# Two transformer blocks on one core: the opening reordered, half of the memory keys moved to the first output stage

## The chip, the cores and the metric

The kernel runs on one core of a Trainium2 chip. The metric is the device time of one execution in microseconds (us). The core has five engines that run side by side, each through its own list of instructions in order: TensorE (PE: matmuls, with its weight loads PEld), VectorE (DVE), ScalarE (ACT), GpSimd (POOL) and SyncE (SP, which here only issues DMAs). Engines wait for each other through semaphores. TensorE writes its results into banks of PSUM; the other engines read them from there into SBUF.

## What is computed

Two blocks follow each other for 512 tokens (S) of width 1024 (D). What matters here is the start of the first block and the memory branch of the second:

```python
def first_block(x, c, positions, w_ada, b_ada, g_pre, w_in, ...):
    mod = silu(c) @ w_ada + b_ada                  # one row of 3 * 1024
    shift, scale, gate = split(mod, 3)
    h = rms_norm(x, g_pre) * (1 + scale) + shift
    proj = h @ w_in                                # qa ka va fa za qb kb vb zb
    oa = forgetting_attention(qa, ka, va, fa + b_fgate) * silu(za)
    ob = sliding_window_sink_attention(rope(qb), rope(kb), vb, sinks) * silu(zb)
    y = concat([oa, ob]) @ w_out
    return x + gate * rms_norm(y, g_post)

def second_block(x, mem, ...):
    h = rms_norm(x, norm_g); mem_h = rms_norm(mem, mem_norm_g)   # mem: 256 tokens
    ...                                            # conv branch, differential attention
    k, v = split(mem_h @ w_mem_kv, 2)              # memory keys and values, 1024 columns each
    k = rms_norm(k per head of 256, kn_g)
    y_mem = (softmax(q @ k.T / 16) @ v * silu(gate)) @ w_proj
    ...
    return x + (g0 * y_conv + g1 * y_diff + g2 * y_mem) @ w_out
```

## The kernel before

**Products.** Most products are made from two halves of each number, a rounded one (`hh`, `wh`: fp32r) and the rest (`hl`, `wl`), as three matmuls: high by high, high by low, low by high. `load_w` (L157) fetches a weight matrix in raw tiles on the SP queue, ACT casts each piece to `wh` (L170), and DVE or POOL subtracts to get `wl` (L172). `mm_T`, `mm_N` and `mm_W` (L202, L213, L221) issue the three matmuls for each of the eight contraction chunks of 128. A few products of the opening are made in plain fp32 instead, where TensorE runs each matmul as two passes: the profile counts a pass as one matmul.

**Order.** In the opening every instruction on PE, ACT, DVE and POOL goes through `Ordered` (L342), which keeps the written order on each engine, so the whole opening shows as line 342. Elsewhere a scheduler places instructions by priority, and may slip them between those of the opening. SP issues DMAs in the written order there.

**The opening** (L346 to L520). It has four strands.

- Memory: `mt` (256 memory tokens) is transposed into `mT`; two chunks of 512 memory-key columns, `mem_k(0)` and `mem_k(1)`, are multiplied in plain fp32 (16 matmuls, so 32 passes each) from raw tiles `rawm` into two PSUM banks `sc`, scaled by ACT into `mk`. `mT` is also written to `mT_d` in memory by a DMA on ACT's queue.
- Tokens: `xn` (512 tokens of 1024) is fetched, its squares summed on ACT, scaled on DVE, transposed by 32 TensorE transposes (`mm<-cst,xn`) and copied by ACT into `xt`.
- Modulation: `w_ada` for shift and scale comes as eight chunks `ada` of 1 MB. For a chunk either ACT and DVE form the products (`products`: two ACT instructions, six of DVE and an add) and TensorE sums over partitions (`sums`: two matmuls with a single column, tile `acc`), or TensorE does all of it (`sums_pe`: 16 matmuls with a single column, tile `ada`). Before, chunks 5 and 7 go the second way. `modulate` makes `mod` and `gs` (0.16 us each on DVE).
- Hidden: `hidden(k)` makes `hh[k]` on ACT, `ht` on DVE and `hl[k]` on POOL (DVE for the last two).

The DMAs are issued on SP in this order: `mt`, the first key chunk's four raw tiles, `ada` 0 and 1, `xn`, two raw tiles of the second key chunk, `ada` 2 and 3, and the rest as buffers come free.

**The first projection** (L644 to L649), `w1c` with 264 columns (kb, vb and the forget gate), follows: 96 matmuls, the token tile outermost, one bank for each of the four token tiles in turn. ACT copies each into `natk`, and DVE makes `fz`. The memory keys are normalised (L555 to L565) at low priority and written to `k_d`. Then the `qb` projection begins (`mm_W`, L221).

**The output stage of the first block** (L923 to L980) runs in two halves of two token tiles (`hf`). In each, `w_out` is applied for two column halves into banks `mm`, ACT and DVE form squares and gated sums (`yq`, `yg`), a norm is applied (L970), ACT squares the result (L972), and `mem_v(hf)` (L906) multiplies one chunk of the memory values, 48 matmuls into two banks of `sc`, which ACT empties into `mv` (L919). The pool of `sc` has two banks.

## Time and profile before

| | before |
|---|---|
| three runs | 1197.31, 1201.15, 1202.04 us (median 1201.15) |
| profiled execution | 1197.03 us, span 1195.2 us |
| mean granted TensorE clock | 0.989 of full speed |
| busy: TensorE | 1157.5 us (97%) |
| busy: VectorE | 883.1 us (74%) |
| busy: ScalarE | 548.6 us (46%) |
| busy: GpSimd | 192.7 us (16%) |

The span is what the profiler saw of the program; the execution's own time is 1.8 us more. A granted clock of 1.00 is 2.4 GHz, 0.50 is 1.2 GHz. Busy time says how long an engine had an instruction in work, not how fast it was. The start of an instruction and the start of the next one on the same engine tell its pace, since TensorE's matmuls overlap.

### The profile page before, as it was taken

The page shows a single profiled execution, that of the slowest core. Times are in us where ns is not written, and L with a number is a line of the kernel's source. Part 1 is how long each engine was busy: PE and PEld are TensorE (multiplying, and loading weights), DVE is VectorE, ACT ScalarE, POOL GpSimd, SP SyncE. Part 2 cuts the span into 40 slices and gives each one's busy share as a digit, 9 for nine tenths or more (in the row PEclk, how much of TensorE's full clock was granted, in tenths as well). Part 3 has the DMA queues.
Part 4 walks back from the last instruction along what each step waited for, and adds up shares of the span by engine and source line. Part 5 has one row for each costly group of instructions (what it writes and reads, how often), then busy time and mean ns, then how long its engine had stood idle before and what let it go on. Part 6 is the DMA issues. An engine that isn't in the chain of part 4 may idle for free.

```text
span 1195.2 us, 16262 instructions
## 1 busy us (share of the span) xinstructions
PE 1157.5 (97%) x5656; PEld 949.9 (79%) x5656; DVE 883.1 (74%) x1910; ACT 548.6 (46%) x1154; POOL 192.7 (16%) x145
## 2 busy tenths in 40 slices
PE   6899999999899999999999999999999999999998
PEld 3677877767588888888887788888888888888887
DVE  4767686658578499999999999999793478454342
ACT  4445665537665454554443643355432245242231
POOL 0233000101122201112020121022011131111100
PEclk9789999999999999999999999999999999999999
DMA  9724222354387323433332443344346855422233
GB/s 366 301 83 147 81 80 82 110 157 122 115 274 236 94 85 105 115 107 104 92 105 88 142 134 113 102 134 136 124 143 201 316 167 201 143 94 96 92 106 106
DMA packets 59073, 167.34 MB, mean 140 GB/s; under 512 B 7056, under 2 KB 10384, under 8 KB 57712
## 3 DMA queue, kind: packets, MB, share of 16 engines
q1 hardware_dynamic: 35968, 123.45, 32.3%
q10 hardware_dynamic: 23024, 42.86, 10.2%
q8 instruction: 44, 0.72, 0.2%
q14 instruction: 37, 0.30, 0.1%
HBM read 137.85 MB, written 21.63 MB: 133 GB/s over the span
## 4 chain that ended last, share of the span: by engine, by line
PE 76%; DVE 17%; issue 2%; ACT 2%; DMA 2%; SPq 0%; ACTq 0%; DVEq 0%
PE mm L202 41%; PE mm L221 18%; DVE cv L1020 6%; PE mm L213 2%; PE sc L221 2%; PE sc L342 2%; DVE wl L172 1%; PE pv L870 1%; PE mm L806 1%; DMA xn<-in_xn_dram 1%; PE pv L1317 1%; PE tp L847 1%; PE tp L342 1%; DVE dp L1140 1%; PE sc L1274 1%
## 5 line engine op out<-in xcount | busy, mean ns | idle before, releaser
L170 ACT CAST wh<-raw 128x512 fp32r<-128x512 f32 (+1 forms) x360 | 214.0, 616 | 203.3 <-PE mm L202 111.9
L172 POOL TENSOR_TENSOR wl<-raw,wh 128x512 fp32r<-128x512 f32 (+1 forms) x90 | 126.8, 1409 | 856.4 <-ACT wh L170 803.4
L172 DVE TENSOR_TENSOR wl<-raw,wh 128x512 fp32r<-128x512 f32 (+1 forms) x270 | 192.0, 723 | 92.7 <-ACT wh L170 89.8
L202 PE MATMUL mm<-hh,wh 128*128 128x512 f32 x640 | 252.1, 394 | 0.0
L202 PE MATMUL mm<-hh,wl 128*128 128x512 f32 x640 | 251.1, 393 | 0.4 <-DVE wl L172 0.4
L202 PE MATMUL mm<-hl,wh 128*128 128x512 f32 x640 | 250.6, 392 | 0.0
L1020 DVE SCALAR_TENSOR_TENSOR cv<-u,vec,cv 128x512 f32<-128x512 f32 x240 | 192.7, 803 | 1.9
L202 PEld LDWEIGHTS mm<-hh,wl 128*128 128x128 f32 x640 | 120.2, 188 | 25.5 <-DVE wl L172 0.6
L202 PEld LDWEIGHTS mm<-hh,wh 128*128 128x128 f32 x640 | 120.3, 188 | 24.0 <-issue 0.5
L202 PEld LDWEIGHTS mm<-hl,wh 128*128 128x128 f32 x640 | 120.3, 188 | 23.8 <-issue 0.2
L221 PE MATMUL mm<-wh,hh 128*128 128x512 f32 x256 | 100.0, 395 | 1.3 <-ACT xqn L1060 1.3
L221 PE MATMUL mm<-wl,hh 128*128 128x512 f32 x256 | 100.8, 394 | 0.3 <-DVE wl L172 0.3
L221 PE MATMUL mm<-wh,hl 128*128 128x512 f32 x256 | 100.5, 395 | 0.0
L202 PE MATMUL mm<-bh,wh 128*128 128x512 f32 x192 | 75.2, 392 | 0.0
L202 PE MATMUL mm<-bh,wl 128*128 128x512 f32 x192 | 74.7, 389 | 0.0
L202 PE MATMUL mm<-bl,wh 128*128 128x512 f32 x192 | 74.7, 389 | 0.0
L1135 ACT ACTIVATE dp<-dp,dst 128x128 f32<-128x128 f32 (+3 forms) x64 | 35.9, 561 | 75.6 <-DVE dst L1133 75.5
L221 PEld LDWEIGHTS mm<-wh,hh 128*128 128x128 f32 x256 | 48.1, 188 | 11.0 <-ACT xqn L1060 1.8
L221 PEld LDWEIGHTS mm<-wl,hh 128*128 128x128 f32 x256 | 48.1, 188 | 10.1 <-DVE wl L172 0.9
L221 PEld LDWEIGHTS mm<-wh,hl 128*128 128x128 f32 x256 | 48.1, 188 | 9.3
L213 PE MATMUL mm<-wh,hh 128*128 128x256 f32 (+1 forms) x160 | 46.1, 292 | 0.0
L213 PE MATMUL mm<-wl,hh 128*128 128x256 f32 (+1 forms) x160 | 45.7, 288 | 0.0
(345 smaller groups left out, 2102.9 us busy)
## 6 DMA issues: line engine op xcount, KB each, us to landing
raw<-in_w_dram SPq DMA_DIRECT2D x88, 512.0 KB
raw<-in_w_out_dram SPq DMA_DIRECT2D x24, 512.0 KB
raw<-in_w2n_dram SPq DMA_DIRECT2D x24, 512.0 KB
ada<-in_w_ada_dram SPq DMA_DIRECT2D x8, 1024.0 KB
rawm<-in_w_mem_dram SPq DMA_DIRECT2D x8, 512.0 KB
raw<-in_w1n_dram SPq DMA_DIRECT2D x8, 512.0 KB
wg<-in_w_gate_dram SPq DMA_DIRECT2D x8, 512.0 KB
raw<-in_w_mem_dram SPq DMA_DIRECT2D x8, 512.0 KB
```

Source lines behind the costliest of these rows:

```text
L170: act.copy(out=wh, in_=raw[:, s])
L172: eng.tensor_tensor(out=wl, in0=raw[:, s], in1=f(wh), op=ALU.subtract)
L202: m = pe.matmul(out=ps, lhsT=a[:, c0:c0 + P], rhs=at(b, k), start=(n == 0 and i == 0), stop=(n == KT - 1 and i == 2))
L213: pe.matmul(out=ps, lhsT=at(a, k)[:, t * P:(t + 1) * P], rhs=b[:, 0:n], start=(start and m == 0 and i == 0), stop=(stop and m == len(order ...
L221: x = pe.matmul(out=ps, lhsT=at(a, k)[:, t * P:(t + 1) * P], rhs=b[:, 0:n], start=(m == 0 and i == 0), stop=(m == KT - 1 and i == 2))
L342: return lambda *a, **k: tc.keep_in_program_order(fn(*a, **k))
L806: m = pe.matmul(out=pm, lhsT=csb[:, 2 * q + k, :], rhs=a[:, k, :], start=(q + k == 0), stop=(2 * q + k == KT - 1))
L847: pe.transpose(out=tp[:, j * P:(j + 1) * P], in_=pt_[:, j * P:(j + 1) * P], identity=ident)
L870: pe.matmul(out=pv[0:64, j * P:], lhsT=l_, rhs=r_[:, j, j * P:], start=(j == 0 and i == 0), stop=(j == NT - 1 and i == 2))
L1020: dve.scalar_tensor_tensor(out=a, in0=u[:, j:j + S], scalar=dw[:, m * 31 + j:m * 31 + j + 1], in1=a, op0=ALU.mult, op1=ALU.add)
L1135: act.activation(out=p_[:, :w], in_=p_[:, :w], func=AF.Exp, scale=-1.0, bias=st_[:, 0, n, m:m + 1], accum_out=st_[:, 1, n, m:m + 1])
L1140: dve.scalar_tensor_tensor(out=pms[0][:, :w], in0=pms[0][:, :w], scalar=rr[:, n, 0:1], in1=pms[1][:, :w], op0=ALU.mult, op1=ALU.add)
```

## The change

- Only the first chunk of memory keys is left in the opening. The second becomes `mem_p(1)`, 48 matmuls of the three-product kind, in the first half of the output stage, right ahead of `mem_p(2)` (the values' first chunk); `mem_p(3)` is in the second half. The norm of the keys is a helper, `mem_k_norm`, called for each chunk. `mv` now has two buffers.
- `xn` is fetched right behind the first chunk's raw tiles, `ada` 0 to 4 after it (five buffers in place of four), `ada` 5, 6 and 7 later.
- Chunks 2, 5 and 7 of the modulation are now `sums_pe`; chunks 0, 1, 3, 4 and 6 are products on ACT and DVE. All eight chunks' sums go to columns of one PSUM tile, `pm`, where each had a tile of its own.
- Two of the four `xn` tiles are scaled on ACT. In `hidden` for chunks 5, 3, 7 and 4, ACT makes `ht` as well as `hh`; POOL makes `hl` but for chunks 4 and 6, where DVE does.
- `w1c` is fetched, cast and multiplied inside the ordered opening: contraction chunk outermost, in the order 0, 1, 2, 5, 3, 7, 4, 6, into four banks at once. `wl` of every second piece is made on POOL. The write of `mT_d` moves from ACT's queue to SP's, behind the `w1c` loads.

```diff
-    def load_w(src, w=CW, rp=None, order=None, on_pool=(3,)):
+    def load_w(src, w=CW, rp=None, order=None, on_pool=(3,), queue=None):
-            nc.sync.dma_start(out=raw, in_=src[:, kq * q:kq * q + kq, :])
+            (queue or nc.sync).dma_start(out=raw, in_=src[:, kq * q:kq * q + kq, :])
...
-        raw_chunk(0, range(4))
-        load_ada(0, 1)
+        for q in range(4):
+            raws.append(pa.tile([P, 2, NW], F32, tag="rawm", name="rawm", bufs=4))
+            sp.dma_start(out=raws[q], in_=A["w_mem"][0][:, 2 * q:2 * q + 2, :])
         for t in range(NT):
             sp.dma_start(out=xn[:, t, :], in_=A["xn"][t])
-        raw_chunk(1, range(2))
-        load_ada(2, 3)
+        load_ada(0, 1, 2, 3, 4)
...
+        pm = tp_tile()
         def sums(k):
-            pms[k] = tp_tile()
             for j in range(2):
-                pe.matmul(out=pms[k][:, j:j + 1], lhsT=accs[k][0][:, j * P:(j + 1) * P], rhs=ones[:, 0:1], start=True, stop=True)
+                pe.matmul(out=pm[:, 2 * k + j:2 * k + j + 1], lhsT=accs[k][0][:, j * P:(j + 1) * P], rhs=ones[:, 0:1], start=True, stop=True)
...
-        def hidden(k, eng):
+        def hidden(k, by, eng):
             t = pa.tile([P, S], F32, tag="ht", name="ht", bufs=2)
             act.activation(out=hh[:, k, :], in_=xt[:, k, :], func=AF.Identity, scale=gs[:, k:k + 1], bias=mod[:, 2 * k:2 * k + 1])
-            dve.tensor_scalar(out=t, in0=xt[:, k, :], scalar1=gs[:, k:k + 1], scalar2=mod[:, 2 * k:2 * k + 1], op0=ALU.mult, op1=ALU.add)
+            if by is act:
+                act.activation(out=t, in_=xt[:, k, :], func=AF.Identity, scale=gs[:, k:k + 1], bias=mod[:, 2 * k:2 * k + 1])
+            else:
+                dve.tensor_scalar(out=t, in0=xt[:, k, :], scalar1=gs[:, k:k + 1], scalar2=mod[:, 2 * k:2 * k + 1], op0=ALU.mult, op1=ALU.add)
             eng.tensor_tensor(out=hl[:, k, :], in0=t, in1=f(hh[:, k, :]), op=ALU.subtract)
...
+        x_transpose(range(KT))
         sums(0)
+        sums_pe(2)
+        load_ada(5, 6, 7)
         sums(1)
+        products(3, act)
         modulate(0)
+        hidden(0, dve, pool)
+        for t in range(2):
+            act.activation(out=mk[:, t, :], in_=kb_[t], func=AF.Copy, scale=mrs[:, t:t + 1])
+        products(3, dve)
         modulate(1)
+        hidden(1, dve, pool)
         products(4, act)
         products(4, dve)
+        modulate(2)
+        hidden(2, dve, pool)
+        sums_pe(5)
         sums(3)
+        sums_pe(7)
         sums(4)
         products(6, act)
+        modulate(5)
+        hidden(5, act, pool)
+        modulate(3)
+        hidden(3, act, pool)
+        w = load_w(A["w1c"], 264, on_pool=(1, 3), queue=sp)
+        sp.dma_start(out=mT_d, in_=mT)
         products(6, dve)
+        modulate(7)
+        hidden(7, act, pool)
         modulate(4)
+        hidden(4, act, dve)
+        wb = [sc_tile(), sc_tile(), pv_tile(), mm_tile()]
+        order = (0, 1, 2, 5, 3, 7, 4, 6)
+        for n, k in enumerate(order):
+            if n == 4:
+                sums(6)
+                modulate(6)
+                hidden(6, dve, dve)
+            wh, wl = w[k]
+            for t in range(NT):
+                for i, (a, b) in enumerate(((hh, wh), (hh, wl), (hl, wh))):
+                    pe.matmul(out=wb[t][:, 0:264], lhsT=a[:, k, t * P:(t + 1) * P], rhs=b, start=(n == 0 and i == 0), stop=(n == KT - 1 and i == 2))
+        mem_k_norm(pa0, mk, 0)
...
-    def mem_v(c, bank):
+    def mem_p(i, bank):
...
-        mv = mvp.tile([P, 2, NW], F32, tag="mv", name="mv")
+        mv = mvp.tile([P, 2, NW], F32, tag="mv", name="mv", bufs=2)
         for t in range(2):
             act.activation(out=mv[:, t, :], in_=banks[t], func=AF.Copy, scale=mrs[:, t:t + 1])
-        nc.scalar.dma_start(out=v_d[:, :, c * NW:(c + 1) * NW], in_=mv)
+        if i == 1:
+            mem_k_norm(mvp, mv, 1)
+        else:
+            nc.scalar.dma_start(out=v_d[:, :, (i - 2) * NW:(i - 1) * NW], in_=mv)
...
-            run(mem_v(hf, sc_tile))
+            for i in ((1, 2), (3,))[hf]:
+                run(mem_p(i, sc_tile))
```

TensorE's list in the kernel before, from the second half of the second key chunk's first tiles to the first matmuls of `w1c` (`sc` from `rawm`: keys; `tp` from `acc`: sums of a modulation chunk; `wh_582`: first piece of `w1c`; a name in brackets is the engine or DMA queue waited for):

```order
L342 MATMUL sc_256<-rawm_152,mT_127 128x512 [waits DMAHW2_49]
L342 MATMUL sc_257<-rawm_152,mT_127 128x512
L342 MATMUL sc_256<-rawm_152,mT_127 128x512
L342 MATMUL sc_257<-rawm_152,mT_127 128x512
L342 MATMUL tp_372<-cst_79,acc_290 128x1 [waits DVE_49]
L342 MATMUL tp_372<-cst_79,acc_290 128x1
L342 MATMUL tp_396<-cst_79,acc_327 128x1 [waits DVE_49]
L342 MATMUL tp_396<-cst_79,acc_327 128x1
L213 MATMUL mm_620<-wh_582,hh_83 128x264 [waits PE_49,Activation_49]
L213 MATMUL mm_620<-wl_583,hh_83 128x264
```

The sums of each chunk had a tile of their own (`tp_372`, `tp_396`), and matmuls of `w1c` lay between them. TensorE's list in the changed kernel, from behind the transposes to the start of `w1c` (`acc_241`, `acc_256`, `acc_341`, `acc_366` are chunks 0, 1, 3 and 4; `ada_149`, `ada_333`, `ada_337` are chunks 2, 5 and 7):

```order
L342 MATMUL tp_155<-cst_79,acc_241 128x1 [waits DMAHW3_49,DVE_49]
L342 MATMUL tp_155<-cst_79,acc_241 128x1
L342 MATMUL tp_155<-cs_106,ada_149 128x1 [waits DMAHW1_49]
L342 MATMUL tp_155<-cs_106,ada_149 128x1 x15
L342 MATMUL tp_155<-cst_79,acc_256 128x1 [waits DVE_49]
L342 MATMUL tp_155<-cst_79,acc_256 128x1
L342 MATMUL tp_155<-cs_106,ada_333 128x1 [waits DMAHW4_49,DVE_49]
L342 MATMUL tp_155<-cs_106,ada_333 128x1 x15
L342 MATMUL tp_155<-cst_79,acc_341 128x1 x2
L342 MATMUL tp_155<-cs_106,ada_337 128x1 [waits DMAHW6_49]
L342 MATMUL tp_155<-cs_106,ada_337 128x1 x15
L342 MATMUL tp_155<-cst_79,acc_366 128x1 x2
```

The keys' second chunk is gone, all sums write the one tile `tp_155`, and every matmul of `w1c` comes after the last of these rows. The first matmul of chunk 5 waits for DVE besides its DMA, and the sums of chunks 3 and 4 have no wait of their own. ACT's list in the changed kernel, from the products of chunk 6 to the casts of `w1c`:

```order
L342 ACTIVATE acc_419<-ada_335,cs_106 128x256 [waits DMAHW5_49,PE_49]
L342 ACTIVATE acc_420<-ada_335,cs_106 128x256
L342 ACTIVATE hh_83<-xt_126,mod_130,gs_129 128x512 [waits DVE_49,Activation_49]
L342 ACTIVATE ht_425<-xt_126,mod_130,gs_129 128x512 [waits Pool_49]
L342 ACTIVATE hh_83<-xt_126,mod_130,gs_129 128x512 [waits DVE_49]
L342 ACTIVATE ht_431<-xt_126,mod_130,gs_129 128x512 [waits Pool_49]
L342 CAST wh_437<-raw_435 128x264 [waits DMAHW7_49]
L342 CAST wh_441<-raw_435 128x264
```

The casts of `w1c` stand behind `hh` and `ht` of chunks 5 and 3 here; in the kernel before they lay between the copies of the transposes. ACT's list in the first half of the output stage, before (`mv`: the emptying of the banks `sc`; `yq_3243` and `yq_3247`: the squares of the two normed token tiles):

```order
L170 CAST wh<-raw 128x512 x7
L972 ACTIVATE yq_3243,ys_3226<-yg 128x1024
L973 DMA x_d<-yg 128x1024
L919 ACTIVATE mv<-sc,mrs 128x512
L951 DMA xs<-in_xn_dram 128x1024
L919 ACTIVATE mv<-sc,mrs 128x512
L972 ACTIVATE yq_3247,ys_3226<-yg 128x1024
```

The same place in the changed kernel, where `mv` is that of the keys' second chunk:

```order
L170 CAST wh<-raw 128x512 x8
L958 ACTIVATE yq_3207,ys_3190<-yg 128x1024
L959 DMA x_d<-yg 128x1024
L937 DMA xs<-in_xn_dram 128x1024
L170 CAST wh<-raw 128x512
L959 DMA x_d<-yg 128x1024
L958 ACTIVATE yq_3211,ys_3190<-yg 128x1024
L902 ACTIVATE mv<-sc,mrs 128x512
L937 DMA xs<-in_xn_dram 128x1024
L902 ACTIVATE mv<-sc,mrs 128x512
```

Both squares and a cast now stand ahead of the first emptying. On TensorE the 48 matmuls of `mem_p(2)` follow those of `mem_p(1)` directly, with nothing between them.

## Rows read from the trace of the kernel before

**Rows 1.** The page's part 1: busy us, share of the span, instructions.

```profile
PE 1157.5 (97%) x5656; PEld 949.9 (79%) x5656; DVE 883.1 (74%) x1910; ACT 548.6 (46%) x1154; POOL 192.7 (16%) x145
```

**Rows 2.** Timeline of TensorE, opening: start us, us, instruction, count, [idle before <-releaser].

```profile
9.97 14.41 PE L342 MATMUL sc<-rawm,mT 128*128 128x512 f32 x32
...
46.36 0.95 PE L342 MATMUL tp<-cst,acc 128*128 128x1 f32 x8
...
52.11 6.96 PE L342 MATMUL tp<-cs,ada 128*128 128x1 f32 x32 [2.32 <-issue]
...
70.92 3.63 PE L342 MATMUL tp<-cs,ada 128*128 128x1 f32 x32
...
84.72 0.62 PE L221 MATMUL mm<-wh,hh 128*128 128x512 f32 x2
...
87.07 0.50 PE L221 MATMUL mm<-wl,hh 128*128 128x512 f32 x1 [0.35 <-DVE wl L172]
```

**Rows 3.** TensorE's groups, 28 to 72 us: line, shapes, count | busy, mean | idle before.

```profile
L342 PE MATMUL sc<-rawm,mT 128*128 128x512 f32 x32 | 20.1, 785 | 5.4 <-ACT mk L342 5.4
```

**Rows 4.** The chain that ended last, opening: start us, us, what.

```profile
8.63 11.21 DMA xn<-in_xn_dram
```

**Rows 5.** Windows, opening: us, busy (x) of PE PEld DVE ACT POOL, PEclk, DMA, GB/s.

```profile
26.00:28.00 2.00, 0.00 (x0) 0.00 (x0) 1.76 (x9) 0.47 (x2) 0.00 (x0) 1.00 1.00 424
...
54.00:56.00 2.00, 2.00 (x11) 2.00 (x11) 2.00 (x3) 0.83 (x3) 1.57 (x2) 0.50 0.00 0
```

**Rows 6.** Timeline of VectorE, opening (columns as in rows 2).

```profile
21.14 2.47 DVE L342 SCALAR_TENSOR_TENSOR acc<-ada,cs,acc 128x256 f32<-128x256 f32 x6 [8.09 <-ACT acc L342]
...
26.48 0.42 DVE L342 TENSOR_TENSOR acc<-acc 128x256 f32<-128x256 f32 x1
...
30.86 2.74 DVE L342 TENSOR_SCALAR xn<-xn,ry 128x1024 f32<-128x1024 f32 x4
...
45.01 1.00 DVE L342 TENSOR_SCALAR ht<-xt,gs,mod 128x512 f32<-128x512 f32 x2
...
53.23 1.52 DVE L342 TENSOR_SCALAR ht<-xt,gs,mod 128x512 f32<-128x512 f32 x1
54.67 3.46 DVE L342 SCALAR_TENSOR_TENSOR acc<-ada,cs,acc 128x256 f32<-128x256 f32 x6
```

**Rows 7.** Timeline of ScalarE, opening (columns as in rows 2).

```profile
36.39 0.91 ACT L342 ACTIVATE acc<-ada,cs 128x256 f32<-128x256 f32 x2 [6.07 <-PE tp L342]
37.21 0.71 ACT L170 CAST wh<-raw 128x264 fp32r<-128x264 f32 x2
37.83 1.06 ACT L342 COPY xt<-mm 128x512 f32<-128x512 f32 x2
...
52.30 1.73 ACT L342 ACTIVATE hh<-xt,mod,gs 128x512 fp32r<-128x512 f32 x2 [3.87 <-DVE gs L342]
```

**Rows 8.** Windows of the first projection's line alone: us, busy of PE, PEld, PEclk, DMA, GB/s.

```profile
76.00:79.00 3.00, 3.00 (x16) 3.00 (x15) 0.50 0.68 210
80.00:83.00 3.00, 3.00 (x26) 2.93 (x25) 1.00 0.39 130
```

**Rows 9.** The chain that ended last, first half of the output stage (columns as in rows 4).

```profile
343.35 12.02 PE mm L221 x53
...
366.95 10.88 PE sc L221 x48
```

**Rows 10.** Timeline of VectorE and ScalarE at the end of `mem_v(0)`.

```profile
342.58 2.48 DVE L970 SCALAR_TENSOR_TENSOR yg<-yg,ry,xs 128x1024 f32<-128x1024 f32 x2
...
343.90 1.06 ACT L972 ACTIVATE yq<-yg 128x1024 f32<-128x1024 f32 x1
...
344.96 0.67 ACT L919 ACTIVATE mv<-sc,mrs 128x512 f32<-128x512 f32 x1
```

**Rows 11.** Timeline of TensorE where the output stage's first matmul waits.

```profile
320.31 0.50 PE L221 MATMUL mm<-wh,ohl 128*128 128x512 f32 x1 [2.04 <-ACT ohl L896]
```

**Rows 12.** Window just after that wait (columns as in rows 5).

```profile
322.00:324.00 2.00, 2.00 (x6) 1.62 (x5) 0.56 (x1) 1.77 (x6) 1.43 (x1) 0.50 0.88 322
```

More of the change, by code (lines that the diff above doesn't have):

```diff
@@ L342, in __getattr__, with mem_k_norm @@
             return lambda *a, **k: tc.keep_in_program_order(fn(*a, **k))
+    def mem_k_norm(wk, mk, c):
+        kss = wk.tile([P, 2, 2], F32, tag="kss", name="kss")
+        kq = wk.tile([P, 256], F32, tag="kq", name="kq")
+        for t in range(2):
+            for h in range(2):
+                act.activation(out=kq, in_=mk[:, t, h * 256:(h + 1) * 256], func=AF.Square, accum_out=kss[:, t, h:h + 1])
+        kr = rsqrt_small(wk, kss.rearrange("p t h -> p (t h)"), 4, 1.0 / 256, 1e-6, "kr")
+        for t in range(2):
+            for h in range(2):
+                s = mk[:, t, h * 256:(h + 1) * 256]
+                dve.tensor_scalar(out=s, in0=s, scalar1=kr[:, t * 2 + h:t * 2 + h + 1], scalar2=None, op0=ALU.mult)
+        nc.scalar.dma_start(out=k_d[:, :, c * NW:(c + 1) * NW], in_=mk)
     mT_d = dram.tile([P, KT, 256], F32, name="mT_d")
@@ L458, in two_block_kernel @@
                     act.activation(out=mT[:, k + j, :], in_=pj, func=AF.Copy, scale=g)
-        mem_k(0, range(KT))
+        kb_ = [sc_tile() for t in range(2)]
+        for k in range(KT):
+            for t in range(2):
+                pe.matmul(out=kb_[t], lhsT=mT[:, k, t * P:(t + 1) * P], rhs=raws[k // 2][:, k % 2, :], start=(k == 0), stop=(k == KT - 1))
         mss = pa.tile([P, 2], F32, tag="mss", name="mss", bufs=1)
@@ L462, in two_block_kernel @@
         squares(mt, mss, range(2))
-        act.dma_start(out=mT_d, in_=mT)
+        dve.tensor_copy(out=mrs, in_=rsqrt_small(pa, mss, 2, 1.0 / 1024, 1e-6, "rn2"))
+        squares(xn, xss, range(NT))
+        r = rsqrt_small(pa, xss, NT, 1.0 / 1024, 1e-6, "rn4")
         products(0, act)
+        for t in range(2):
+            dve.tensor_scalar(out=xn[:, t, :], in0=xn[:, t, :], scalar1=r[:, t:t + 1], scalar2=None, op0=ALU.mult)
+            act.activation(out=xn[:, t + 2, :], in_=xn[:, t + 2, :], func=AF.Copy, scale=r[:, t + 2:t + 3])
         products(0, dve)
@@ L467, in two_block_kernel @@
         products(1, dve)
-        load_ada(4)
-        dve.tensor_copy(out=mrs, in_=rsqrt_small(pa, mss, 2, 1.0 / 1024, 1e-6, "rn2"))
-        squares(xn, xss, range(NT))
-        mem_k_out(0)
-        mem_k(1, range(2))
+        x_transpose(range(KT))
         sums(0)
+        sums_pe(2)
+        load_ada(5, 6, 7)
         sums(1)
-        r = rsqrt_small(pa, xss, NT, 1.0 / 1024, 1e-6, "rn4")
-        for t in range(NT):
-            dve.tensor_scalar(out=xn[:, t, :], in0=xn[:, t, :], scalar1=r[:, t:t + 1], scalar2=None, op0=ALU.mult)
+        products(3, act)
@@ L504, in two_block_kernel @@
+        w = load_w(A["w1c"], 264, on_pool=(1, 3), queue=sp)
+        sp.dma_start(out=mT_d, in_=mT)
         products(6, dve)
+        modulate(7)
+        hidden(7, act, pool)
         modulate(4)
-        hidden(4, pool)
-        modulate(5)
-        hidden(5, pool)
-        mem_k(1, range(4, 7))
-        sums(6)
-        mem_k(1, range(7, 8))
-        mem_k_out(1)
-        sums_pe(7)
-        modulate(6)
-        hidden(6, dve)
-        modulate(7)
-        hidden(7, dve)
+        hidden(4, act, dve)
```

76 lines of the change are left out of this document (13 added, 63 removed).

## The prediction

> **What bounds the kernel now.** I read the busy times first, then TensorE's timeline through the opening, then the chain that ended last. TensorE is busy for 97% of the span [rows 1], so it sets the time, and a change can gain only where TensorE is idle, runs at half clock, or does work that can be dropped. The opening is such a place: the `qb` projection, from which on TensorE is nearly always fed, begins at 84.72 and has a wait of its own of 0.35 us a little later [rows 2], so the comparable point is 84.72 + 0.35 = 85.1. The two key chunks take 14.41 us [rows 2] and 20.1 us there, the second after 5.4 us without work [rows 3]. Eight chunks' sums, two of them by `sums_pe` at 6.96 and 3.63 us, fill in [rows 2]. The output stage is the other kind: TensorE has work there nearly all the time, so what is added there is paid for.
>
> **The opening, step by step.** The sum is a time for the comparable point in the changed kernel.
>
> First keys: unchanged, 9.97 + 14.41 = 24.4 [rows 2]. The transposes behind them need scaled `xn`. It landed at 8.63 + 11.21 = 19.8 [rows 4], and two `ada` chunks of 1 MB, 2.1 million bytes, that stood ahead of it now stand behind it: 4.9 us less at 424 GB/s [rows 5], so about 14.9. Four squares of about 1.06 (an ACT square of the same size [rows 10]) and ten small DVE steps, some 2 us, reach 21; scaling two of the four tiles on each of DVE and ACT takes 2.74 / 2 = 1.4 [rows 6]. Ready by about 22.5, the scaling is hidden under the keys; without the earlier landing it would have ended at 27.
>
> Transposes: ACT's copies pace them, eight at 1.06 / 2 [rows 7]: 4.2, to 28.6. The `mT_d` DMA no longer holds ACT's list; it stands on SP behind loads that nobody waits for later, so it costs nothing. Then `sums(0)`, `sums_pe(2)` at full clock and `sums(1)`: 0.95 / 2 + 3.63 + 0.95 / 2 = 4.6 [rows 2], to 33.2.
>
> Now the step on which most rests. All sums write one tile, so DVE's reading of it (`modulate(2)`) has to come before the next write (`sums_pe(5)`): the order shows that matmul waiting for DVE. Queued behind it on TensorE are chunks 3, 7 and 4 and all of `w1c`. DVE has ahead of `modulate(2)`: `modulate(0)` 0.4, `ht` 0.5, products of chunk 3 at 2.47 + 0.42, `modulate(1)` 0.4, `ht` 0.5, products of chunk 4 at 2.47 + 0.42 [rows 6], `modulate(2)` 0.4. Beside them POOL makes `hl`: six such products took 3.46 in place of 2.47 with POOL at work [rows 6, 5], so 1.0 for the first set and, with less overlap, 0.6 for the second. ACT's `hh` at 1.73 / 2 and first product of chunk 4 at 0.46 [rows 7] let the second set start about 0.8 later than DVE alone would. Sum 0.4 + 0.5 + 2.9 + 1.0 + 0.4 + 0.5 + 0.8 + 2.9 + 0.6 + 0.4 = 10.4, but the second wait for ACT and the slower products partly coincide; I take 10.1, to 43.3. TensorE is idle for these 10 us.
>
> The Trainium skill, page "SBUF — State Buffer", section "Who interferes with whom", has a rule against this arrangement: VectorE with two SBUF inputs and GpSimd exclude each other for a whole instruction, and the later one stands still. The trace agrees, with a `tensor_scalar` of 1.52 us where two took 1.00 [rows 6]. By that rule the two sets would lose a full `hl` each in the worst case, about half a us more in the sum; by the measured row they lose the 1.0 and 0.6 above.
>
> After such a pause the clock is low: after an idle of 2.32 us [rows 2] the granted clock was 0.50 and `sums_pe` did not raise it [rows 5]. So I take `sums_pe(5)` and `sums_pe(7)` at 6.96 each and two `sums` at 0.9: 15.7, to 59.0. Bounds: 3.63 for each if the clock rises at once (6.7 less), 3.3 more if `sums_pe(2)` too falls to half clock.
>
> Then `modulate(5)`, 0.4; four ACT instructions for chunks 5 and 3, which now stand ahead of the casts, 4 x 0.87 = 3.5; one cast 0.36 [rows 7]: `w1c` starts at about 63.2. In the kernel before, its casts were done between the transposes' copies. Its 96 matmuls take 3.00 / 25 = 0.12 each at full clock, or about 0.2 at half [rows 8]: 11.7, and 2.3 for some five us at half clock. The fourth raw tile waits for a buffer, which POOL's `wl` frees about 65, then for its DMA and cast, and through products 6, `modulate(7)`, `hh`, `ht` and POOL's `hl`, chunk 7 is ready at about 75; TensorE reaches it, sixth in order, near 74. I allow 1 us for that (0 to 4), and 0.5 for `sums(6)`. End: 63.2 + 11.7 + 2.3 + 1.0 + 0.5 = 78.7.
>
> The opening gains 85.1 - 78.7 = **6.4 us**. The key norm and the emptying of the banks lie on ACT and DVE beside `qb`; if their cover fails, that is a us or less.
>
> **The output stage.** The 48 matmuls added cost 10.88 us [rows 9]; the removed fp32 passes are already in the opening's sum. A wait is added. The pool `sc` has two banks; `mem_p(2)`, right behind, needs those of `mem_p(1)`, which ACT empties (`mv`) only after both squares `yq`, since the scheduler put them first. Before, the matmuls of `mem_v(0)` ended at 343.35 [rows 9], while DVE finished the second `yg` at 342.58 + 2.48 = 345.06 [rows 10]. The square of it, 1.06, and an `mv`, 0.67 [rows 10], end at 346.8: TensorE waits 346.8 - 343.35 = 3.5 (4.4 with a cast in between; 0 if the norm there is done sooner). Queued behind on TensorE is all of the rest. After a wait of 2.04 [rows 11] the clock was at half for a stretch of 3.4 us around the window shown [rows 12]; that costs half of it, 1.7 (0 to 3.4). Sum 10.9 + 3.5 + 1.7 = **16.1 us**.
>
> Weight tiles are no limit there: DMA, ACT and DVE have slack at that point, and the raw bytes are those that the opening no longer loads.
>
> **Net:** 16.1 - 6.4 = +9.7 us on the profiled execution of 1197.03, or 1206.7. That execution is at the low end of what was timed: the three runs have a median of 1201.15, and with the profiled one a mean of 1199.4. The changed kernel's runs will scatter likewise; 1199.4 + 9.7 = **1209**. About 0.5% (6 us) is what a measurement of this kernel can tell from no change.
>
> **Rivals.**
> (1) *The one tile does not hold TensorE.* If writes to other columns of `pm` need not wait for `modulate(2)`, `sums_pe(5)` and `sums_pe(7)` run as their data lands, at full clock, right behind 33.2: 33.2 + 2 x 3.63 + 0.9 = 41.4. DVE's list still ends with `modulate(2)` at 43.3; then `modulate(5)`, four ACT instructions and a cast, 0.4 + 3.5 + 0.4, start `w1c` near 47, 16 us sooner than in my sum. Gain 6.4 + 16 = 22 against 16.1: -6, 1193, **faster**. It decides if the wait for DVE at that matmul ends before about 36. Against it: the order names DVE as waited for.
> (2) *The bank wait does not arise.* If the norm of `yg` is early enough for `mv` to be done while `mem_p(1)`'s last matmuls run, only 10.9 is paid: +4.5, about 1204, within 0.5%. For it: before, `mem_v(0)`'s matmuls were mixed with those of `w_out`; without that mixing `w_out` ends sooner and its norm with it. Against: the distance of 3.5 is larger than the 1.8 us or so of mixing.
> (3) *The opening gives nothing.* If the fourth raw tile comes late, `w1c` stays at half clock (96 x 0.08 = 7.7 in place of 2.3) and chunk 7 holds it for 2 more, the gain is eaten: +16, about 1215.
>
> **How the numbers follow.** My forecast (+7 to +12, 1206 to 1211) gets 0.51, rival 1 0.09, rival 2 0.22, rival 3 0.18. The range is from 1199, which leaves out rival 1 and the lower edge of rival 2 with quick runs, to 1217, which takes in rival 3 with both bounds of the output stage. Within 0.5% means 1195.1 to 1207.2: most of rival 2 and the lower edge of the forecast, 0.28. Faster: rival 1, 0.09. Slower: 0.63.
>
> **What would show it.** In the profile of the changed kernel: transposes starting right at the end of the first keys, near 24.4; TensorE idle for about 10 us before the third long `tp<-cs,ada` group or the second, released by DVE; that group and the next at about 7 us each with a granted clock of 0.50; the first `w1c` matmul near 63 and `qb` near 79; 96 matmuls `sc<-` one after another in the output stage with a wait of 3 to 4 us for ACT's `mv` in their middle, and half clock behind it. I am wrong if TensorE's wait for DVE in the opening is short, if `sums_pe` runs at full clock there, or if no wait splits the 96 matmuls.

## The result

| | before | after |
|---|---|---|
| runs, beside each other | 1197.31 to 1202.04 us, median 1200.12 (4) | 1212.89 to 1217.15 us, median 1215.07 (4) |
| ratio of the times, 95% interval | 1 | 1.0131 [1.0104, 1.0157] |
| profiled execution, span | 1197.03 us, 1195.2 us | 1217.15 us, 1215.4 us |
| mean granted TensorE clock | 0.989 | 0.976 |

The changed kernel is slower by 15 us, on the side that was forecast and within the range of 1199 to 1217, but 6 us above the predicted 1209 and outside the narrower forecast of 1206 to 1211. Its page's part 1 (busy us, share of the span, instructions) answers to [rows 1]:

```profile
PE 1163.2 (96%) x5700; PEld 964.6 (79%) x5700; DVE 887.2 (73%) x1909; ACT 559.2 (46%) x1180; POOL 199.9 (16%) x149
```

TensorE's busy time grew by 5.7 us and the span by 20.2: most of the loss is idle time, not work. TensorE's timeline of the opening in the changed kernel (start us, us, instruction, count, [idle before <-releaser]) answers to [rows 2]:

```profile
24.10 3.89 PE L342 MATMUL mm<-cst,xn 128*128 128x128 f32 x32
...
28.20 4.50 PE L342 MATMUL tp<-cs,ada 128*128 128x1 f32 x32
...
43.80 6.99 PE L342 MATMUL tp<-cs,ada 128*128 128x1 f32 x32 [10.24 <-DVE mod L342]
...
51.50 6.96 PE L342 MATMUL tp<-cs,ada 128*128 128x1 f32 x32
...
63.41 0.59 PE L342 MATMUL sc<-wh,hh 128*128 128x264 f32 x1 [4.09 <-ACT wh L342]
64.74 0.59 PE L342 MATMUL sc<-wl,hh 128*128 128x264 f32 x1 [0.74 <-DVE wl L342]
...
74.22 0.61 PE L342 MATMUL tp<-cst,acc 128*128 128x1 f32 x4 [1.89 <-DVE mod L342]
```

The transposes follow the keys with no pause; chunk 2 runs at once; then 10.24 us of nothing until DVE has done `modulate(2)`; chunks 5 and 7 take twice what a chunk takes at full clock; `w1c` starts at 63.41.

**A ledger.** Line 202's matmuls (`mm_T`) are the same in both kernels and in the same order, so the nth of one can be set against the nth of the other. Its first, TensorE in the kernel before and then in the changed one:

```profile
109.90 0.48 PE L202 MATMUL mm<-hh,wh 128*128 128x512 f32 x1
```

```profile
106.76 0.48 PE L202 MATMUL mm<-hh,wh 128*128 128x512 f32 x1
```

Its first behind the output stage, in the same order:

```profile
412.82 0.40 PE L202 MATMUL mm<-hh,wh 128*128 128x512 f32 x1
```

```profile
429.86 0.40 PE L202 MATMUL mm<-hh,wh 128*128 128x512 f32 x1
```

| place | after less before, us |
|---|---|
| first matmul of line 202, behind the opening | -3.14 |
| 361st, ahead of the output stage | -3.02 |
| 401st, behind the output stage | +17.03 |
| last | +20.13 |

So the opening gave 3.1 us back and the output stage took 20.05. The last 3.1 are not shown to belong to the change: in the profiles of the eleven other kernels below the same stretch moved by -0.6 to +4.7 us, and the changed kernel's profile has a stretch of half clock there that before's has not (granted clock 0.51 from 795.5 to 799). The profiled execution of before is also 3 us under the median of its runs and that of the changed kernel 2 us above, so the medians differ by 15 where the two profiles differ by 20.

Below, "opening" is the first of these lags for one profiled execution of a kernel, always against the profile of before, and "stage" is what the lag grows by from the 361st to the 401st. The ratios come from all runs and need not be the ratio of the two medians.

### The profile page after: what moved, and what is told of

It reads as the page before. It is cut to its first block, busy times and chain, and to the rows that moved or that the text cites. A ratio compares the mean times of both kernels' runs of the same rounds, so it can differ in the third digit from the quotient of the medians.

```text
span 1215.4 us, 16379 instructions
## 1 busy us (share of the span) xinstructions
PE 1163.2 (96%) x5700; PEld 964.6 (79%) x5700; DVE 887.2 (73%) x1909; ACT 559.2 (46%) x1180; POOL 199.9 (16%) x149
## 4 chain that ended last, share of the span: by engine, by line
PE 75%; DVE 17%; issue 3%; DMA 2%; ACT 2%; POOL 0%; ACTq 0%; SPq 0%; DVEq 0%; POOLq 0%
PE mm L202 42%; PE mm L221 15%; DVE cv L1007 6%; PE sc L221 2%; PE tp L342 2%; PE mm L213 2%; DVE wl L172 2%; PE sc L342 1%; PE pv L853 1%; PE mm L789 1%; DMA raw<-in_w_mem_dram 1%; PE tp L830 1%; PE pv L1304 1%; DVE acc L342 1%; DVE dp L1120 1%
## 5 line engine op out<-in xcount | busy, mean ns | idle before, releaser
L170 ACT CAST wh<-raw 128x512 fp32r<-128x512 f32 x360 | 216.7, 620 | 207.3 <-PE mm L202 111.7
L172 POOL TENSOR_TENSOR wl<-raw,wh 128x512 fp32r<-128x512 f32 x90 | 132.2, 1469 | 860.2 <-ACT wh L170 797.1
L172 DVE TENSOR_TENSOR wl<-raw,wh 128x512 fp32r<-128x512 f32 x270 | 199.4, 751 | 96.8 <-ACT wh L170 93.1
L202 PE MATMUL mm<-bh,wh 128*128 128x512 f32 x192 | 75.3, 392 | 0.0
L202 PEld LDWEIGHTS mm<-bl,wh 128*128 128x128 f32 x192 | 36.1, 188 | 7.7 <-issue 0.2
L202 PEld LDWEIGHTS mm<-bh,wh 128*128 128x128 f32 x192 | 36.1, 188 | 7.6 <-issue 0.2
```

The lines of the kernel that those rows point to most:

```text
L170: act.copy(out=wh, in_=raw[:, s])
L172: eng.tensor_tensor(out=wl, in0=raw[:, s], in1=f(wh), op=ALU.subtract)
L202: m = pe.matmul(out=ps, lhsT=a[:, c0:c0 + P], rhs=at(b, k), start=(n == 0 and i == 0), stop=(n == KT - 1 and i == 2))
```

## The experiments

**Does the one tile hold TensorE?** Chunks 5, 6 and 7 get a second PSUM tile, and `sums_pe(5)` and `sums_pe(7)` go ahead of `sums(3)` and `sums(4)`:

```diff
-        pm = tp_tile()
+        pa_, pb_ = tp_tile(), tp_tile()
+        pms = {k: pb_ if k in (5, 6, 7) else pa_ for k in range(KT)}
...
         sums_pe(5)
-        sums(3)
         sums_pe(7)
+        sums(3)
         sums(4)
```

> The changed kernel with the sums of modulation chunks 5, 6 and 7 in a second PSUM tile, and the TensorE sums of chunks 5 and 7 right behind each other, ahead of those of chunks 3 and 4. Theory (the one tile holds TensorE until VectorE has read chunk 2): TensorE's idle 10.24 us before chunk 5 shrinks to the landing of that chunk's data (1 to 4 us), the first matmul of the first projection comes near 48 us where it was at 63.4, and the time falls by 10 to 15 us, to 1200 to 1205. Rival (the opening is set by the products on VectorE and ScalarE, the wait on TensorE only shows it): the first projection starts earlier but waits inside for chunks 3, 7, 4 and 6, and the time falls by 3 us or less, to 1212 or above.

Measured: 1200.38 us (median of 10), 1.0013 [0.9994, 1.0032] of before, and 14.7 below the changed kernel. TensorE's timeline of the opening:

```profile
33.92 13.79 PE L342 MATMUL tp<-cs,ada 128*128 128x1 f32 x64
...
52.69 0.59 PE L342 MATMUL sc<-wh,hh 128*128 128x264 f32 x1 [3.26 <-ACT wh L342]
```

The 64 passes of chunks 5 and 7 start 10 us earlier, without a wait for DVE, and `w1c` starts 10.7 us earlier (at 52.69, where 48 was expected). They still take 13.79 us, the slow clock's price (granted clock 0.51 from 33 to 48), so the wait goes and the clock doesn't come back with it. Opening -15.7, stage +18.1. The tile is the cause of the pause.

**Does the bank wait cost the output stage 10 us?** The banks of `mem_p(1)` come from another pool:

```diff
-                run(mem_p(i, sc_tile))
+                run(mem_p(i, mm_tile if i == 1 else sc_tile))
```

> The changed kernel with the two banks of the moved key chunk taken from the pool of the output projection (mm), so that the values' chunk behind it does not wait for them to be emptied. Theory (the wait is for the banks, emptied late on ScalarE behind both squares): the 6.42 us of idle between the two chunks and the 6.8 us at half clock behind it (3.4 us lost) go, the time falls by 8 to 10 us, to 1205 to 1207. Rival (the casts and the loads of the values' weights are late as well, 0.52 us of waiting for a load stands on ScalarE there): TensorE waits for the weights instead, the idle time stays above 3 us and the time falls by 4 us or less.

Measured: 1210.62 us (4), 1.0096 [1.0060, 1.0132]; 4.5 below the changed kernel, stage 17.3 in place of 20.05. In the changed kernel the long wait of TensorE in this stage was:

```profile
347.06 0.80 PE L221 MATMUL sc<-wh,mh 128*128 128x512 f32 x1 [6.42 <-ACT mv L902]
```

With other banks that wait is gone, and TensorE's timeline shows four others, all for weights:

```profile
331.41 0.50 PE L221 MATMUL mm<-wl,mh 128*128 128x512 f32 x1 [0.73 <-DVE wl L172]
...
344.28 0.50 PE L221 MATMUL sc<-wl,mh 128*128 128x512 f32 x1 [0.79 <-DVE wl L172]
...
352.53 0.74 PE L221 MATMUL sc<-wh,mh 128*128 128x512 f32 x2 [1.06 <-ACT wh L170]
...
359.33 0.50 PE L221 MATMUL mm<-wl,ohl 128*128 128x512 f32 x1 [1.03 <-DVE wl L172]
```

The chain that ended last names the first link of the third:

```profile
344.25 7.59 DMA raw<-in_w_mem_dram
351.86 0.63 ACT wh L170
```

Two matrices right behind each other ask for weights faster than they come: a raw tile took 7.59 us here. With a fifth of 0.30 the waits sum to 3.9 in place of 6.42, and the half clock behind the long wait, worth 2.5, is gone too (granted clock 1.00 from 340 to 370). That makes 5.0, but the stage falls by 2.7: 1.3 of the rest is lost in the attention ahead of the output projection, which the edit doesn't touch (its first matmul behind the wait for `ohl` starts at 318.91 in place of 317.32, and 0.3 of that was there at the 361st), and 1.0 is not accounted for. Neither theory fits alone: the banks were the longest wait, and behind it stood the weights, which I had written off as no limit.

**Is the late piece of `w1c` a matter of raw tiles?** The opening's four `rawm` buffers, free by then, take the raw tiles of `w1c` in place of three others (the fourth, for the last two pieces, had to wait for one of the three):

```diff
-            raw = rp.tile([P, kq, w], F32, tag="raw", name="raw", bufs=4) if rp else wp.tile([P, kq, w], F32, tag="raw", name="raw", bufs=3)
+            raw = rp.tile([P, kq, NW], F32, tag="rawm", name="raw", bufs=4)[:, :, 0:w] if rp else wp.tile([P, kq, w], F32, tag="raw", name="raw", bufs=3)
...
-        w = load_w(A["w1c"], 264, on_pool=(1, 3), queue=sp)
+        w = load_w(A["w1c"], 264, rp=pa, on_pool=(1, 3), queue=sp)
```

> The changed kernel with the raw tiles of the first projection's weights in four buffers (the four that the first key chunk leaves free) in place of three. Theory (the fourth raw tile, loaded only after a buffer came free at 65.3 and cast at 69.6, holds the products of chunk 6 on VectorE, and with them TensorE at the sums of chunk 6): the idle 1.89 us there and the half clock from 75.3 to 78.7 (1.7 us lost) go, 2 to 4 us in all, 1211 to 1213. Rival (the products of chunk 6 are late for another reason, or hh and hl of chunk 7 hold TensorE next): less than 1 us.

Measured: 1210.55 us (4), 1.0098 [1.0061, 1.0135]; 4.5 less than the changed kernel. The opening's part is 3.25 (its first line-202 matmul starts at 103.51 in place of 106.76); by the 361st only 1.0 of it is left in the profiles, so the rest of the 4.5 is not shown to come from the raw tiles. The windows from 74 to 78 us (busy us of PE, PEld, DVE, ACT, POOL, then granted clock, DMA share, GB/s), first of the changed kernel, then of this one, show where:

```profile
74.00:78.00 4.00, 3.78 (x21) 3.78 (x22) 1.17 (x6) 3.94 (x7) 1.27 (x1) 0.66 0.73 244
```

```profile
74.00:78.00 4.00, 4.00 (x31) 3.77 (x30) 3.64 (x7) 2.99 (x7) 1.61 (x2) 1.00 0.65 263
```

In the changed kernel the wait of 1.89 us is followed by half clock, and 21 matmuls fit where 31 do without it. The wait is a DMA's: in its chain the tile lands late, and `wl`, products of chunk 6 and `modulate(7)` queue up behind it on DVE:

```profile
65.32 4.22 DMA raw<-in_w1c_dram
69.56 0.42 ACT wh L342
```

```profile
70.01 0.43 DVE L342 TENSOR_TENSOR wl<-raw,wh 128x264 fp32r<-128x264 f32 x1 [3.53 <-ACT wh L342]
70.36 3.02 DVE L342 SCALAR_TENSOR_TENSOR acc<-ada,cs,acc 128x256 f32<-128x256 f32 x6
```

**What does the moved key chunk do by itself?** The kernel before, with nothing but `mem_p`, the norm of the keys in two halves and the first-half placement taken over; its opening is the old one, without the second key chunk:

```diff
-        mem_k(1, range(2))
...
-        mem_k(1, range(2, 4))
...
-            run(mem_v(hf, sc_tile))
+            for i in ((1, 2), (3,))[hf]:
+                run(mem_p(i, sc_tile))
```

> The kernel before with the second key chunk moved to the output stage and nothing else of the change: its loads and fp32 matmuls are out of the opening, and mem_p is that of the changed kernel. Theory (in the opening the key passes mostly filled time in which TensorE waits for the modulation): the opening ends only 3 to 8 us earlier, the output stage pays about 20 us as in the changed kernel, the time is 1212 to 1217, about that of the changed kernel. Rival (the 20.1 us of key passes are on the path of the opening): it ends some 20 us earlier, the time is about 1200, and it is the other reorderings of the change that cost.

Measured: 1208.99 us (10), 1.0079 [1.0057, 1.0102]. Opening -9.9, stage +19.0. The chunk's 20.1 us of TensorE's time [rows 3] bring 9.9 when they go, and cost 19 where they come. The rest of the reordering, with one tile, then gives back 6.8 of those 9.9 (opening -3.1); with two tiles it adds 5.8 to them (-15.7).

**And the reordering without the chunk?** The changed kernel without `mem_p(1)`: the second half of the keys isn't computed, and the first is written in its place.

```diff
+        nc.scalar.dma_start(out=k_d[:, :, NW:2 * NW], in_=mk)
...
-            for i in ((1, 2), (3,))[hf]:
+            for i in ((2,), (3,))[hf]:
```

> The changed kernel without the moved chunk: the second half of the memory keys is left out and the first half is written in its place. Theory: the time falls by what the output stage paid in the profile, 10.88 us of matmuls, 6.4 of idle and 3.4 at half clock less some 0.6 elsewhere, 20 us, to about 1195; the opening's gain of 3 us is then all that is left against the kernel before. Rival (part of the stall in the output stage is there without the moved chunk, since the norm on VectorE is late anyway): it falls by 12 to 16 us, to 1200 or above.

Measured: 1201.00 us (10), 1.0014 [0.9991, 1.0038]: the chunk costs 14.1 in the changed kernel, 10.88 of it for the matmuls, as the rival had it. The stage still stands 7.4 above before in the profile, though nothing is added to it. That profile is the slowest of this kernel's runs, 7 above its median; it has one weight wait of 2.67 us with a raw tile of 8.47 ahead of it.

**Can the chunk sit in the pause?** The changed kernel with its second key chunk back in the opening, as 16 fp32 matmuls between `sums(1)` and `sums_pe(5)`:

```diff
+        kb1 = [mm_tile() for t in range(2)]
+        for k in range(KT):
+            for t in range(2):
+                pe.matmul(out=kb1[t], lhsT=mT[:, k, t * P:(t + 1) * P], rhs=raws1[k // 2][:, k % 2, :], start=(k == 0), stop=(k == KT - 1))
         sums_pe(5)
...
-            for i in ((1, 2), (3,))[hf]:
+            for i in ((2,), (3,))[hf]:
```

> The changed kernel with the move of the keys undone: the second key chunk is back in the opening as 16 fp32 matmuls, put where TensorE is idle for 10.24 us (behind the sums of chunk 1), its raw tiles loaded behind modulation chunk 4. One sum tile as in the change. Theory (that idle time and the half clock behind it were unused): the 14.4 us of key passes cost 4 us more than the gap, the two TensorE sums behind them run at full clock and give back 6.7, and the output stage's 20 us go: the time falls by 18 to 24 us against the changed kernel, to 1191 to 1197, below the kernel before. Rival (raw tiles and modulation chunks 5 and 7 land later by 4.9 us and hold TensorE, the clock stays low): the opening ends 5 to 10 us later than in the changed kernel, the time is 1200 to 1205.

Measured: 1202.21 us (10), 1.0027 [1.0006, 1.0047]; opening -3.5, of which 0.9 is left by the 101st matmul of line 202. TensorE's timeline:

```profile
32.99 15.60 PE L342 MATMUL mm<-rawm,mT 128*128 128x512 f32 x32
48.43 3.63 PE L342 MATMUL tp<-cs,ada 128*128 128x1 f32 x32
...
52.37 6.09 PE L342 MATMUL tp<-cs,ada 128*128 128x1 f32 x32
...
63.41 0.59 PE L342 MATMUL sc<-wh,hh 128*128 128x264 f32 x1 [4.10 <-ACT wh L342]
```

15.60 us of keys are in, and `w1c` starts at 63.41, to the hundredth as without them. They fill a pause of 10.24, and the chunks behind them win the rest back, since the clock is full for chunk 5 (3.63 in place of 6.99) and for a part of chunk 7 (6.09 in place of 6.96). So the key passes cost nothing up to `w1c`. What follows them is not free: at the 101st matmul this kernel is 2.4 us behind the changed one, with a wait of 1.50 for a `wl` of DVE at 108.62, whose list now holds the norm of the second key half too. The total fell by 13, not by the 18 to 24 expected, because of these 2.4 and because the stage stays 5.0 above before without anything added in it.

**Both: keys in the pause, and two tiles.** The edits of the first and the last experiment together.

> As the run before, with the second sum tile for chunks 5, 6 and 7. Theory (with the keys in the gap TensorE no longer waits for VectorE there, so the second tile has nothing left to free): within 3 us of the run before. Rival (the one tile still costs, through the order of the sums): 5 us or more below it.

Measured: 1209.04 us (5), 1.0086 [1.0055, 1.0116]. With the pause filled, the second tile frees nothing: TensorE's timeline has the keys in 16.58 us, chunks 5 and 7 in 11.38 (3.63 + 6.09 with one tile), and `w1c` at 65.63, 2.2 later. Neither expectation held: the time is 6.8 above the run before, of which the profiles show 2.2 in the opening and 3.6 in the stage, where the second tile plays no part.

```profile
32.87 16.58 PE L342 MATMUL mm<-rawm,mT 128*128 128x512 f32 x32
49.28 11.38 PE L342 MATMUL tp<-cs,ada 128*128 128x1 f32 x64
...
65.63 0.59 PE L342 MATMUL sc<-wh,hh 128*128 128x264 f32 x1 [3.26 <-ACT wh L342]
```

**Is there a version that beats both?** Four were tried. First the second tile, the other banks and the four raw tiles together:

> The changed kernel, keys in the output stage, with all three single edits: second sum tile, other banks, four raw tiles. Theory (the three costs are in different places and add up, less a part of the raw tile's that the second tile already freed): 1215.1 less 14.7, 4.5 and 1 to 3, that is 1193 to 1196. Rival (they overlap, the weights in the output stage take what the banks give): 1198 to 1200.

Measured: 1200.56 us (10), 0.9995 [0.9974, 1.0017]; opening -13.6, stage +13.6. The opening pays for the stage exactly, and the three gains of 14.7, 4.5 and 4.5 don't add: all of them together give what the second tile gives alone. Then the same, with three raw buffers of their own for the memory weights and the norm of the second key half at low priority:

```diff
-        w = load_w(A["w_mem"][i], NW)
+        w = load_w(A["w_mem"][i], NW, rp=mvp)
...
-            mem_k_norm(mvp, mv, 1)
+            with low(LOWMK):
+                mem_k_norm(mvp, mv, 1)
```

> The run with three edits (second sum tile, other banks, four raw tiles) and two more in the output stage: the memory weights have three raw buffers of their own, and the norm of the moved keys has low priority. Theory (what the output stage still pays above the 10.88 us of matmuls, 2.7 us in that run's profile, are waits for weights whose raw tiles queue behind the output projection's): 2 to 3 us less than that run's 1200.6, about 1198. Rival (raw buffers are not what holds the weights; casts and subtractions are): no change, 1200 to 1201.

Measured: 1199.80 us (10), 1.0026 [1.0006, 1.0045] against the runs of before beside it (median 1199.48); no gain, and in its profile the stage stands at +16.1 where it was +13.6. Then those buffers, with the key chunk in the output stage's second half, behind the values:

```diff
-            with low(LOWMK):
-                mem_k_norm(mvp, mv, 1)
+            mem_k_norm(mvp, mv, 1)
...
-            for i in ((1, 2), (3,))[hf]:
-                run(mem_p(i, mm_tile if i == 1 else sc_tile))
+            for i in ((2,), (3, 1))[hf]:
+                run(mem_p(i, sc_tile))
```

> As the run before in buffers (second sum tile, four raw tiles, own raw buffers for the memory weights), with the moved key chunk put in the second half of the output stage, behind the values' second chunk, in the banks sc. Theory (the stall comes from the norm of the token tiles standing ahead of the emptying; in the second half it is longer, since the transposes of the last tokens follow): TensorE waits there again, 3 to 6 us, the time is 1201 to 1205. Rival (the last norm hides behind the added matmuls, where TensorE waited before): below 1198.

Measured: 1203.07 us (10), 1.0042 [1.0020, 1.0064]; stage +19.2, with a wait for weights of 2.23 us and one of 1.87 for `mv`, shorter than the 3 to 6 expected. Last the keys in the pause with one tile, four raw tiles, and the values as before but from raw buffers of their own:

```diff
-        w = load_w(A["w1c"], 264, on_pool=(1, 3), queue=sp)
+        w = load_w(A["w1c"], 264, rp=pa, on_pool=(1, 3), queue=sp)
...
-    def mem_p(i, bank):
+    def mem_v(c, bank):
...
-        w = load_w(A["w_mem"][i], NW)
+        w = load_w(A["w_mem"][2 + c], NW, rp=mvp)
```

> The changed opening with one sum tile, the second key chunk back in TensorE's idle time there, four raw tiles for the first projection, the values' code of the kernel before with three raw buffers of its own. Theory (keys in the gap cost nothing there, the raw tiles give 3 us, and the output stage is that of the kernel before again): the opening ends 3 to 4 us earlier than in the kernel before, the output stage is within 2 us, the time is 1195 to 1199. Rival (the order that the scheduler gives the output stage shifts with what stands ahead, and costs 5 to 8 us as in the two runs with the keys in the gap): 1201 to 1206.

Measured: 1201.24 us (8), 1.0034 [1.0015, 1.0054]; its stage is down to +2.9, but TensorE idles 2.93 us ahead of the keys, runs at half clock from 31.1 to 41.3, and the opening ends 1.4 later than before's. None beats the kernel before.

Times, and the lags behind the kernel before at the four places of the ledger:

| kernel | us | ratio | first | 361st | 401st | last |
|---|---|---|---|---|---|---|
| changed | 1215.07 | 1.0131 | -3.1 | -3.0 | +17.0 | +20.1 |
| two tiles | 1200.38 | 1.0013 | -15.7 | -15.7 | +2.3 | +1.7 |
| other banks | 1210.62 | 1.0096 | -3.3 | -2.7 | +14.6 | +15.3 |
| four raw tiles | 1210.55 | 1.0098 | -6.4 | -4.0 | +15.6 | +15.3 |
| before, key chunk moved alone | 1208.99 | 1.0079 | -9.9 | -9.6 | +9.4 | +10.7 |
| second key half left out | 1201.00 | 1.0014 | -3.1 | -1.2 | +6.3 | +11.0 |
| keys in the pause | 1202.21 | 1.0027 | -3.5 | -0.5 | +4.5 | +5.2 |
| keys in the pause, two tiles | 1209.04 | 1.0086 | -1.3 | +1.3 | +9.9 | +10.2 |
| two tiles, other banks, four raw tiles | 1200.56 | 0.9995 | -13.6 | -13.5 | 0.0 | -0.3 |

## Why the prediction held, and where it was off

**What held.** The one tile was the right thing to rest it on. TensorE idled for 10.24 us (10.1 in the sum) until DVE finished `modulate(2)` at 43.74 (43.3); chunks 5 and 7 took 6.99 and 6.96 (6.96 each); `w1c` started at 63.41 (63.2). Two small errors cancel on the way: the transposes ended at 28.0 (28.6), and chunk 2 took 4.50 (3.63). The 6.96 was right for another reason than the one given. I put the low clock down to the pause, but it had fallen at 30.9, among the matmuls of chunk 2 and ahead of the pause, and in the two-tile run, which has no pause there, it was at half as well. That part is luck. DVE's timeline shows the terms, the two product sets beside POOL and the `modulate` that released TensorE:

```profile
34.51 3.47 DVE L342 SCALAR_TENSOR_TENSOR acc<-ada,cs,acc 128x256 f32<-128x256 f32 x6
...
40.04 3.17 DVE L342 SCALAR_TENSOR_TENSOR acc<-ada,cs,acc 128x256 f32<-128x256 f32 x6 [0.76 <-ACT acc L342]
...
43.59 0.15 DVE L342 SCALAR_TENSOR_TENSOR mod<-tp,vec 128x2 f32<-128x2 f32 x1
```

The sets lost 1.0 and 0.7 to POOL against the 2.47 of [rows 6] (1.0 and 0.6 in the sum). POOL's timeline has the two `hl` beside them:

```profile
34.93 1.58 POOL L342 TENSOR_TENSOR hl<-ht,hh 128x512 fp32r<-128x512 f32 x1 [34.48 <-ACT hh L342]
39.69 1.26 POOL L342 TENSOR_TENSOR hl<-ht,hh 128x512 fp32r<-128x512 f32 x1 [3.18 <-ACT hh L342]
```

The Trainium skill, page "SBUF — State Buffer", section "Who interferes with whom", has VectorE with two SBUF inputs and a GpSimd instruction that reads SBUF exclude each other for a whole instruction. The second `hl` began 0.35 ahead of its set, so by that rule it could hold the set for 0.91, and the first for about 1.26. The trace's 0.7 and 1.0 lie 0.2 to 0.3 below: it agrees in the main. The row that the prediction gave for it, a `tensor_scalar`, reads one tensor and two columns of scalars, and is no case of two tensor inputs.

Rival 1 is out by the two-tile run: the tile did hold TensorE, and without it the kernel is as fast as before. The 22 us that it gave the opening were too many: the two-tile kernel gained 15.7 there, since chunks 5 and 7 stayed at half clock. Rival 2 is out by the wait itself. Its mixing was also smaller than the 1.8 us it was put at: in the kernel before four matmuls of `w_out` stand between those of `mem_v(0)`, 0.9 us.

**The opening's last term was too small.** In the sum the opening gave 6.4; it gave 3.1. To `w1c`'s start the sum was good to 0.2. Behind it, 1 us was allowed for the late piece (0 to 4), and this is the term that failed: 0.74 for the first `wl`, which the sum didn't have, 1.89 of wait at `sums(6)`, and half clock from 75.3 to 78.7, worth 1.7. That makes 0.2 + 0.74 + 1.89 + 1.7 - 1.0 = 3.5 lost of 6.4. The cause was named (the fourth raw tile, through products of chunk 6 and `modulate(7)`), but its place was off: I looked at chunk 7, where TensorE would wait near 74, and the pause came at `sums(6)`, whose matmuls stand one chunk ahead of it. (The products of chunk 6 were done at 73.83; the last 0.4 of the wait is again the one tile, which two `modulate` still had to read.) The four-raw-tile run takes the pause away and gets 3.25 back. So rival 3 was partly true. Its 1215 is the time that was measured, but by chance: it gave the opening no gain and the output stage its forecast cost, where the opening kept 3.1 and the output stage took 4 more.

**The output stage's wait was mis-sized.** 16.1 in the sum, 20.05 measured: 10.88 for the matmuls as foreseen, 6.42 of wait in place of 3.5, and 2.5 for half clock in place of 1.7 (the 48 matmuls behind the wait took 13.36 in place of 10.88). The windows behind the wait, columns as above:

```profile
344.00:348.00 4.00, 0.94 (x2) 0.83 (x3) 3.40 (x12) 3.48 (x9) 0.00 (x0) 0.62 1.02 391
348.00:352.00 4.00, 4.00 (x11) 3.11 (x10) 3.90 (x6) 2.02 (x9) 1.28 (x1) 0.53 1.02 410
```

TensorE was idle for most of the first window, where a low clock costs nothing, and the clock stood at 0.53 in the second. (The expectations of the other-banks run and of the run without the chunk counted 3.4, half of the whole stretch of 6.8 at half clock, with the idle time in it.) The terms add to 19.8 against the 20.05 of the ledger.

The wait was too short in the sum because the emptying came late, not because the matmuls ended early. To set times of the two profiles beside each other the lag of 3.0 has to come off: TensorE's wait for `ohl` ends at 320.31 [rows 11] and at 317.32. `mem_p(1)` ended at 340.6, and the 343.35 of the sum [rows 9] becomes 340.4. DVE's second `yg` ended at 344.25, where 345.06 [rows 10] becomes 342.1: the norm was 2.2 late. ACT's list then ran as the order had it; its timeline:

```profile
343.09 1.06 ACT L958 ACTIVATE yq<-yg 128x1024 f32<-128x1024 f32 x1 [0.45 <-DVE yg L956]
...
344.76 0.62 ACT L170 CAST wh<-raw 128x512 fp32r<-128x512 f32 x1 [0.52 <-DMA raw<-in_w_mem_dram]
345.28 1.05 ACT L958 ACTIVATE yq<-yg 128x1024 f32<-128x1024 f32 x1
346.34 1.24 ACT L902 ACTIVATE mv<-sc,mrs 128x512 f32<-128x512 f32 x2
```

A cast that waits 0.52 for its DMA stands between the squares (the sum had it as a bound of 4.4, outside its 3.5), so the second square began 1.0 behind its `yg`, and `mv` comes last. 2.2 and 1.0, less the 0.2 by which `mem_p(1)` ended later, are the 3 us that were missing. Behind both stand weights. The chain that ended last runs through two raw tiles, the first ahead of the norm's first step on DVE (`rv`), the second ahead of that cast:

```profile
331.02 3.83 DMA raw<-in_w_mem_dram
...
334.87 0.63 ACT wh L170
...
335.52 0.69 DVE wl L172
336.21 1.21 DVE rv L236
...
341.01 3.65 DMA raw<-in_w_mem_dram
```

DVE stood idle for 1.46 us ahead of that `wl`, which its list has in front of `rv`; that is the larger part of the 2.2, and slower steps of the norm are the rest. The prediction had written off weight tiles as no limit there. That is the step that failed: the changed kernel's own trace refutes it, and the other-banks run shows the same from the other side. The first of the two tiles could be fetched only when DVE had freed its buffer, at 331.0, and DVE was slow at that time. Its timeline and POOL's:

```profile
324.69 8.11 DVE L172 TENSOR_TENSOR wl<-raw,wh 128x512 fp32r<-128x512 f32 x5 [2.22 <-ACT wh L170]
```

```profile
324.12 4.62 POOL L895 TENSOR_TENSOR ml<-ml,mh 128x2048 fp32r<-128x2048 f32 x1 [0.50 <-ACT mh L894]
```

Five `wl` took 8.11 us beside POOL's `ml`, a step that the sum didn't have; in the kernel before the same `ml` ended at 327.16, ahead of DVE's first `wl` there at 327.71.

**The sum.** 16.1 - 6.4 = 9.7 was forecast; the ledger has 20.05 - 3.0 = 17 up to the end of the output stage, and the medians differ by 15. Both steps erred to the same side, 3.3 and 4 us, by stalls that a list of durations doesn't show: pieces of weight that land late, and half clock behind the two pauses that they make.

**What stays open.** Without the key chunk the output stage should cost what it cost before, and it stood 7.4, 5.0 and 8.6 above it in three profiles. What TensorE waited for there is known: a cast of weights for 2.67 us in the first and 3.43 in the third, DVE's `hn` for 1.72 in the second, with half clock behind each. Why these came late is not known. The order of casts, squares and `mv` there differs from before's, as the scheduler's list depends on what stands ahead. In the last version, with raw buffers of their own for the values, the stage stood at 2.9, but such buffers brought no gain where they were added to the three edits. That this order is the cause is argued, not shown.

## What to carry to other kernels

Several results in one PSUM tile can tie a write of the tile to earlier readers of it: here a matmul of one chunk waited 10.24 us for VectorE's reading of another, and a second tile was worth 14.7 us. Before work is moved out of a stage, ask whether it fills a pause: 15.60 us of key passes in the opening's pause cost nothing up to the next product and 2.4 us behind it, and the same product cost 14.1 where TensorE was busy. Where two products follow each other on a pool of two banks, look at the list of the engine that empties the banks, and then at whether the weights of both can come that fast.
